# Summing the squares of the SSD branch's outputs on GpSimd over the feature blocks, and on TensorE once at the branch's end

## The chip, the cores and the metric

One core of one Trainium2 chip runs the whole program. The metric is the device time of one execution in microseconds (us). A core has five engines that run side by side: PE (TensorE, matrix products; its weight loads are shown apart as PEld), DVE (VectorE), ACT (ScalarE), POOL (GpSimd) and SP (which only issues DMA transfers here; ACT issues a few as well). Each engine works through its own list of instructions in a fixed order, and waits in place when something that the next instruction needs is not there yet. TensorE's clock has two levels, 1.2 and 2.4 GHz; the profile gives the granted clock as a share of the full one.

## The reference, cut to what matters

The program is a network of five layers over 512 positions of width 1024. The change is in the first layer, in its state-space branch (SSD). That branch gates its output and normalises it over 2048 features:

```python
def ssd_output(y, xs, z, d_skip, g):
    Bsz, L = y.shape[:2]
    y = y + d_skip.reshape(SSD_GROUPS, SSD_HPG, 1).astype(y.dtype) * xs
    return rmsnorm(y.reshape(Bsz, L, D_SSD) * jax.nn.silu(z), g)

def rmsnorm(x, g):
    x32 = x.astype(jnp.float32)
    y = x32 * lax.rsqrt(jnp.mean(x32 * x32, axis=-1, keepdims=True) + EPS)
    return (y * g.astype(jnp.float32)).astype(x.dtype)
```

So each of the 512 positions needs the sum of the squares of 2048 gated features. The factor that comes of it is multiplied in later, behind the branch's output product.

## The kernel before, in words

All is float32. Activations lie with features on the 128 partitions and positions along a row, so 2048 features are 16 blocks of [128, 512]. Large products are made of three products of split operands (`mm3`, lines L101 to L103).

`ssd` handles the branch in four groups of four feature blocks. For each group, `_ssd_project` makes the inputs (PSUM tiles `px`), `_ssd_gate` the gates (`pz`, then `z`), `_ssd_scan` the recurrence over four chunks, forward and backward (state products `pst`, outputs of the state `pof`, diagonal products `pyd`, states `S`, result `y`), and `_ssd_finish` ends the group. While the scan of a group runs, its own gates and the next group's projections are fed in between as filler; in the last group the filler is the attention output product (`pa`) of the class `Mixer`.

`_ssd_finish` does this for each of four blocks j: four transposes of `y` into one PSUM tile `pyT` (the pool `K.pm` has one buffer here), a product with the gate on DVE (L1940), the square on ACT (`sq`, one buffer, L1942), four products on PE that sum the square over the partitions into a [128, 4] tile `pss` (L1944), the scaling by the norm's gain on ACT (L1946), and a write to DRAM (`yd`, issued by ACT, L1947). After the four blocks DVE adds `pss` to `ssy` (L1948). A float32 product is two instructions on PE, so four products show as eight.

When the branch is done, `Mixer.run` turns `ssy` into a row factor (L1997 and after), loads the 16 blocks back (`oin` from `yd`, issued by SP, L1962) and goes on with the weights of the output products.

The order of the instructions on each engine is not written by hand. The framework's scheduler sets it, once, when the program is built, by simulating the whole program in time; so an edit in one place can move instructions in others. Tiles are reused through pools: a new tile waits until the readers of the old one are done. `psum` in `ssd` has one buffer for each tag, and `pst`, `pof` and the chunk product `pcb` share the tag `s`.

Of the kernel before, what the change touches and what calls it, by code (L numbers as in the profile page):

```python
# [9 lines left out]
F32 = mybir.dt.float32  # L10
# [3 lines left out]
ALU = mybir.AluOpType  # L14
# [4 lines left out]
P = 128  # L19
D = 1024  # L20
L = 512
# [1726 lines left out]
def ssd(K, XL, XC, W, V, YD, ssy, last):  # L1748

    nc, tc = K.nc, K.tc
    with ExitStack() as cx:
        pool = cx.enter_context(tc.tile_pool(name="ss", bufs=1))
        psum = cx.enter_context(tc.tile_pool(name="ssp", bufs=1, space=PSUM))
        nc.vector.memset(ssy, 0.0)
        cur = {}
        for _ in _ssd_project(K, pool, XL, XC, W, V, 0, cur):
            pass
        for g in range(4):  # L1760
            nxt, zs = {}, []
            fill = _chain(_ssd_gate(K, pool, XL, W, g, zs), _ssd_project(K, pool, XL, XC, W, V, g + 1, nxt) if g < 3 else last)
            y = pool.tile([P, 4, L], F32, tag="y", bufs=1, name=K.nm("y"))
            for _ in _ssd_scan(K, pool, psum, V, g, cur, y):
                next(fill, None)
            for _ in fill:
                pass
            _ssd_finish(K, pool, psum, V, g, y, zs, YD, ssy)
            cur = nxt


def _chain(*parts):
    for p in parts:
        yield from p
# [49 lines left out]
def _ssd_gate(K, pool, XL, W, g, zs):  # L1824

    nc = K.nc
    for j in range(4):
        w = K.w(W["w_z"][g * 4 + j], [P, KD, P])
        p = K.pg.tile([P, L], F32, tag="g", name=K.nm("pz"))
        K.gemm(p, w, XL, 0)  # L1830
        z = pool.tile([P, L], F32, tag="z", bufs=4, name=K.nm("z"))
        nc.scalar.activation(z, p, AF.Tanh, scale=0.5)
        nc.vector.scalar_tensor_tensor(z, z, 1.0, p, op0=ALU.add, op1=ALU.mult)
        zs.append(z)
        yield
# [93 lines left out]
        yield  # L1929


def _ssd_finish(K, pool, psum, V, g, y, zs, YD, ssy):
    nc = K.nc
    pss = psum.tile([P, 4], F32, tag="q", name=K.nm("pss"))
    for j in range(4):
        z = zs[j]
        pt = K.pm.tile([P, 4, P], F32, tag="m", name=K.nm("pyT"))
        for c in range(4):
            nc.tensor.transpose(pt[:, c, :], y[:, c, j * P:(j + 1) * P], K.ident)
        nc.vector.tensor_tensor(z, pt.rearrange("p a b -> p (a b)"), z, op=ALU.mult)  # L1940
        sq = pool.tile([P, L], F32, tag="sq", bufs=1, name=K.nm("sq"))
        nc.scalar.activation(sq, z, AF.Square)  # L1942
        for c in range(4):
            nc.tensor.matmul(pss[:, c:c + 1], sq[:, c * P:(c + 1) * P], K.ones[:, 0:1],  # L1944
                             start=j == 0 and c == 0, stop=j == 3 and c == 3)
        nc.scalar.activation(z, z, AF.Copy, scale=V["ng"][:, g * 4 + j:g * 4 + j + 1])  # L1946
        nc.scalar.dma_start(YD[g * 4 + j], z)  # L1947
    nc.vector.tensor_tensor(ssy, ssy, pss, op=ALU.add)  # L1948


class Mixer:
# [237 lines left out]
def network(ctx, tc, A, out):  # L2189
# [50 lines left out]
    with ExitStack() as c1:  # L2240
# [33 lines left out]
        with ExitStack() as c2:  # L2274
            K.open_ps(c2, 2, 1)
            K.pump_every, K.pool_w = 2, (2,)
            M = Mixer(K, sub("M"), YD, AD, GD, ssy)
            ssd(K, XL, XC, sub("S"), VS, YD, ssy, M.attention_part(c_x))
# [131 lines left out]
```

## Time and profile before

| | us |
|---|---|
| median of 3 runs | 4372.11 (4363.34 to 4372.17) |
| the profiled execution's own time | 4365.29 |
| its span in the profile | 4363.5 |
| mean granted TensorE clock | 0.952 |
| PE busy | 4007.8 (92%) |
| DVE busy | 2739.3 (63%) |
| ACT busy | 1751.1 (40%) |
| POOL busy | 1507.5 (35%) |

The SSD branch ends at about 1025 us of the span. Busy shares are means over stages that have different limits, and PE's busy time is modelled, since products are pipelined. The sums below are made against the profiled execution, whose own time is 6.8 us under the median.

### The profile page before, as it was taken

How to read it: one execution, taken by the hardware profiler on the slowest of the kernel's cores; microseconds unless marked ns; L12 is line 12 of the kernel's file. 1: busy time of each engine (PE TensorE's matmuls, PEld its weight loads, DVE VectorE, ACT ScalarE, POOL GpSimd, SP SyncE). 2: the span in 40 equal slices, each digit the busy share in tenths (PEclk: the TensorE clock that was granted, in tenths of full speed). 3: DMA queues.
4: the chain of work that ended last, by engine and by line, in shares of the span. 5: the costliest groups of instructions: out<-in, count | busy, mean ns of one | idle time of the engine just before them, and what ended most of it. 6: DMA issues, size and time to landing. Idle time of an engine off the chain costs nothing. (4 is left out here: it accounts for less than half of the span.)

```text
span 4363.5 us, 67568 instructions
## 1 busy us (share of the span) xinstructions
PE 4007.8 (92%) x26396; PEld 3288.7 (75%) x26396; DVE 2739.3 (63%) x4361; ACT 1751.1 (40%) x3331; POOL 1507.5 (35%) x1046
## 2 busy tenths in 40 slices
PE   5888999988989999999988989789989999999999
PEld 3766767656766779888977777577777888888987
DVE  6455476676788884445786687865555466663433
ACT  4445445432233334223343555333323465543321
POOL 4333144443444442222344544534411222211221
PEclk7999999988999999999988998899999999999999
DMA  5113121235444553324534667745512311122222
GB/s 190 60 57 99 54 83 51 85 116 169 145 147 150 168 190 117 97 87 139 174 121 158 222 196 225 188 120 143 139 57 92 102 48 51 53 95 92 90 94 87
DMA packets 345550, 518.45 MB, mean 119 GB/s; under 512 B 114424, under 2 KB 217464, under 8 KB 343696
## 3 DMA queue, kind: packets, MB, share of 16 engines
q1 hardware_dynamic: 339040, 502.08, 37.4%
q10 hardware_dynamic: 6192, 12.06, 0.8%
q8 instruction: 208, 3.41, 0.3%
q14 instruction: 110, 0.90, 0.1%
HBM read 425.86 MB, written 88.19 MB: 118 GB/s over the span
## 5 line engine op out<-in xcount | busy, mean ns | idle before, releaser
L93 POOL TENSOR_TENSOR wlo<-raw,whi 128x1024 fp32r<-128x1024 f32 (+2 forms) x254 | 569.6, 2243 | 1332.8 <-ACT whi L91 960.8
L91 ACT ACTIVATE whi<-raw 128x1024 fp32r<-128x1024 f32 (+3 forms) x399 | 383.4, 962 | 706.4 <-PE pz L102 132.2
L95 DVE TENSOR_TENSOR wlo<-raw,whi 128x1024 fp32r<-128x1024 f32 (+3 forms) x278 | 350.2, 1261 | 288.4 <-ACT whi L91 282.1
L127 DVE SCALAR_TENSOR_TENSOR macc<-mraw,conds,macc 128x1024 f32<-128x1024 f32 x168 | 272.0, 1634 | 36.8 <-DMA mraw<-mw 36.5
L103 PE MATMUL pu<-xh,wlo 128*128 128x512 f32 x608 | 243.0, 400 | 10.3 <-DVE wlo L95 6.5
L102 PE MATMUL pu<-xl,whi 128*128 128x512 f32 x608 | 242.1, 398 | 1.1 <-DVE xl L258 1.1
L101 PE MATMUL pu<-xh,whi 128*128 128x512 f32 x608 | 240.4, 399 | 2.9 <-DVE fu L2063 2.4
L89 DVE CAST whi<-raw 128x1024 fp32r<-128x1024 f32 (+2 forms) x133 | 99.5, 748 | 150.1 <-PE pz L102 46.6
L226 POOL TENSOR_TENSOR rsr<-rsv,mhalf 128x4 f32<-128x4 f32 (+3 forms) x56 | 77.9, 1391 | 276.3 <-DVE rsv L224 258.7
L102 PE MATMUL pz<-xl,whi 128*128 128x512 f32 x384 | 150.0, 391 | 0.0
L101 PE MATMUL pv<-whi,xh 128*128 128x256 f32 x512 | 139.0, 283 | 7.0 <-ACT whi L91 6.2
L103 PEld LDWEIGHTS pu<-xh,wlo 128*128 128x128 f32 x608 | 116.0, 191 | 39.0 <-DVE wlo L95 7.3
L102 PE MATMUL pv<-wlo,xh 128*128 128x256 f32 x512 | 142.1, 282 | 0.0
L103 PE MATMUL pv<-whi,xl 128*128 128x256 f32 x512 | 140.2, 282 | 0.5 <-DVE xl L258 0.5
L101 PEld LDWEIGHTS pu<-xh,whi 128*128 128x128 f32 x608 | 116.1, 191 | 31.8 <-issue 3.5
L102 PEld LDWEIGHTS pu<-xl,whi 128*128 128x128 f32 x608 | 116.0, 191 | 29.1 <-DVE xl L258 1.8
L102 PE MATMUL po<-slo,whi 128*128 128x512 f32 (+1 forms) x384 | 136.1, 357 | 0.0
L103 PE MATMUL po<-shi,wlo 128*128 128x512 f32 (+1 forms) x384 | 135.4, 357 | 0.0
L101 PE MATMUL po<-shi,whi 128*128 128x512 f32 (+1 forms) x384 | 133.9, 364 | 0.5 <-ACT shi L111 0.5
L992 PE MATMUL pgm<-ar,kb 128*128 128x256 f32 x384 | 116.8, 427 | 18.9 <-DMA ar<-fe 15.7
L334 POOL TENSOR_TENSOR u<-u,z 128x512 f32<-128x512 f32 (+1 forms) x48 | 58.5, 1218 | 165.2 <-DVE z L325 165.2
L101 PE MATMUL pl<-xlh,whi 128*128 128x512 f32 x208 | 93.3, 452 | 13.2 <-DVE rp L1488 10.2
(747 smaller groups left out, 12923.8 us busy)
## 6 DMA issues: line engine op xcount, KB each, us to landing
mraw<-mw SPq DMA_DIRECT2D x128, 512.0 KB
raw<-G_wuz SPq DMA_DIRECT2D x96, 512.0 KB
raw<-G_wv SPq DMA_DIRECT2D x48, 512.0 KB
raw<-G_wout SPq DMA_DIRECT2D x48, 512.0 KB
raw<-F_w_up SPq DMA_DIRECT2D x44, 512.0 KB
raw<-R_w_in SPq DMA_DIRECT2D x70, 256.0 KB
raw<-S_w_xbc SPq DMA_DIRECT2D x24, 512.0 KB
fe<-ra SPq DMA_DIRECT2D x16, 768.0 KB
```

Of the source, the lines that this page charges most:

```text
L89: nc.vector.tensor_copy(hi, raw)
L91: nc.scalar.activation(hi, raw, AF.Copy)
L93: nc.gpsimd.tensor_tensor(lo, raw, hi.bitcast(F32), op=ALU.subtract)
L95: nc.vector.tensor_tensor(lo, raw, hi.bitcast(F32), op=ALU.subtract)
L101: nc.tensor.matmul(ps, a[0], b[0], start=start, stop=False)
L102: nc.tensor.matmul(ps, a[0], b[1], start=False, stop=False)
L103: return nc.tensor.matmul(ps, a[1], b[0], start=False, stop=stop)
L127: nc.vector.scalar_tensor_tensor(acc, raw, c[:, kt:kt + 1], acc, op0=ALU.mult, op1=ALU.add)
L226: nc.gpsimd.tensor_tensor(r, v, self.mhalf[:, :n], op=ALU.pow)
L334: nc.gpsimd.tensor_tensor(u, u, z, op=ALU.mult)
L992: nc.tensor.matmul(pgm[:, d], kb[:, i, d, :], ar[:, i, d], start=True, stop=True)
```

## The change

The squares are no longer summed over the partitions one by one. The first block's square is written straight into a new tile `acc` (named `yss`, [128, 512]), and POOL adds each of the other 15 squares to it. After the fourth group four products sum `acc` over the partitions, into a PSUM tile `pss` of the tag `s`, and DVE copies it to `ssy`. The tag `q` of the PSUM pool, the clearing of `ssy` and the four adds to it are gone.

```diff
--- before.py
+++ after.py
@@ -1753,8 +1753,7 @@
     with ExitStack() as cx:
         pool = cx.enter_context(tc.tile_pool(name="ss", bufs=1))
         psum = cx.enter_context(tc.tile_pool(name="ssp", bufs=1, space=PSUM))
-        nc.vector.memset(ssy, 0.0)
-        cur = {}
+        acc, cur = pool.tile([P, L], F32, name="yss"), {}
         for _ in _ssd_project(K, pool, XL, XC, W, V, 0, cur):
             pass
         for g in range(4):
@@ -1765,8 +1764,12 @@
                 next(fill, None)
             for _ in fill:
                 pass
-            _ssd_finish(K, pool, psum, V, g, y, zs, YD, ssy)
+            _ssd_finish(K, pool, V, g, y, zs, YD, acc)
             cur = nxt
+        pss = psum.tile([P, 4], F32, tag="s", name=K.nm("pss"))
+        for c in range(4):
+            nc.tensor.matmul(pss[:, c:c + 1], acc[:, c * P:(c + 1) * P], K.ones[:, 0:1], start=True, stop=True)
+        nc.vector.tensor_copy(ssy, pss)
 
 
 def _chain(*parts):
@@ -1929,23 +1932,21 @@
         yield
 
 
-def _ssd_finish(K, pool, psum, V, g, y, zs, YD, ssy):
+def _ssd_finish(K, pool, V, g, y, zs, YD, acc):
+
     nc = K.nc
-    pss = psum.tile([P, 4], F32, tag="q", name=K.nm("pss"))
     for j in range(4):
         z = zs[j]
         pt = K.pm.tile([P, 4, P], F32, tag="m", name=K.nm("pyT"))
         for c in range(4):
             nc.tensor.transpose(pt[:, c, :], y[:, c, j * P:(j + 1) * P], K.ident)
         nc.vector.tensor_tensor(z, pt.rearrange("p a b -> p (a b)"), z, op=ALU.mult)
-        sq = pool.tile([P, L], F32, tag="sq", bufs=1, name=K.nm("sq"))
+        sq = acc if g == j == 0 else pool.tile([P, L], F32, tag="sq", bufs=1, name=K.nm("sq"))
         nc.scalar.activation(sq, z, AF.Square)
-        for c in range(4):
-            nc.tensor.matmul(pss[:, c:c + 1], sq[:, c * P:(c + 1) * P], K.ones[:, 0:1],
-                             start=j == 0 and c == 0, stop=j == 3 and c == 3)
+        if sq is not acc:
+            nc.gpsimd.tensor_tensor(acc, acc, sq, op=ALU.add)
         nc.scalar.activation(z, z, AF.Copy, scale=V["ng"][:, g * 4 + j:g * 4 + j + 1])
         nc.scalar.dma_start(YD[g * 4 + j], z)
-    nc.vector.tensor_tensor(ssy, ssy, pss, op=ALU.add)
 
 
 class Mixer:
```

In the listings of the changed kernel a line number from L1785 to L1947 is three higher than that of the same line before.

PE, at the end of the first group, from the second group's first state product to the next gate's product `pz`. Before:

```order
L1857 MATMUL pst_5471<-x_1148_5469,BTc_4739 128x512
L1939 MATMUL pyT_5411<-ident,y_4429 128x128 x4
L1857 MATMUL pst_5477<-x_1151_5475,BTc_4739 128x512
L1939 MATMUL pyT_5425<-ident,y_4429 128x128 x4
L1944 MATMUL pss_5410<-ones,sq_5417 128x1 x4
L1857 MATMUL pst_5484<-x_1154_5482,BTc_4739 128x512
L1939 MATMUL pyT_5439<-ident,y_4429 128x128 x4
L1944 MATMUL pss_5410<-ones,sq_5431 128x1 x4
L1857 MATMUL pst_5490<-x_1157_5488,BTc_4739 128x512
L1939 MATMUL pyT_5453<-ident,y_4429 128x128 x4
L1944 MATMUL pss_5410<-ones,sq_5445 128x1 x4
L101 MATMUL pz_5634<-xlh_184,whi_5630 128x512
```

After the change, from the same place:

```order
L1860 MATMUL pst_5455<-x_1146_5453,BTc_4739 128x512
L1942 MATMUL pyT_5410<-ident,y_4429 128x128 x4
L1860 MATMUL pst_5461<-x_1149_5459,BTc_4739 128x512
L1942 MATMUL pyT_5419<-ident,y_4429 128x128 x4
L1860 MATMUL pst_5468<-x_1152_5466,BTc_4739 128x512
L1942 MATMUL pyT_5430<-ident,y_4429 128x128 x4
L1860 MATMUL pst_5474<-x_1155_5472,BTc_4739 128x512
L1942 MATMUL pyT_5441<-ident,y_4429 128x128 x4
L101 MATMUL pz_5618<-xlh_184,whi_5614 128x512
```

The three `pss` rows are gone; a fourth, which stood inside the gate's product, is gone too. The state products `pst` and the transposes `pyT` now follow each other directly.

POOL, at the same place: `x_...` is an input of a state product, `S` a state scaled by its decay. Before:

```order
L1855 TENSOR_TENSOR x_1157_5488<-xTc_4737,wd 128x512
L1862 TENSOR_TENSOR S_5674<-S_5479,ex 128x512
L1862 TENSOR_TENSOR S_5492<-S_5486,ex 128x512
L1862 TENSOR_TENSOR S_6359<-S_5492,ex 128x512
L1909 TENSOR_TENSOR dm_5539<-dm_5539,cbs_5531 128x512
L1909 TENSOR_TENSOR dm_5602<-dm_5602,cbs_5531 128x512
```

After the change:

```order
L1858 TENSOR_TENSOR x_1155_5472<-xTc_4737,wd 128x512
L1865 TENSOR_TENSOR S_5658<-S_5463,ex 128x512
L1947 TENSOR_TENSOR yss<-yss,sq_5425 128x512
L1865 TENSOR_TENSOR S_5476<-S_5470,ex 128x512
L1947 TENSOR_TENSOR yss<-yss,sq_5436 128x512
L1865 TENSOR_TENSOR S_6343<-S_5476,ex 128x512
L1947 TENSOR_TENSOR yss<-yss,sq_5447 128x512
L93 TENSOR_TENSOR wlo_5903<-raw_5900,whi_5902 128x1024
```

The adds into `yss` now stand between the state scalings; one of them stands ahead of `S_5476` (before: `S_5492`), the last state that the second group's start needs. On PE the product `pcb`, with which the second group's first chunk starts, stands behind 24 instructions of the gate's product now; before it stood behind 15.

PE, at the end of the fourth group, from the last filler product `pa` on. Before:

```order
L103 MATMUL pa_8264<-ox_7887,wlo_8272 128x512
L1870 MATMUL pof_8110<-S_8104,CF_6822 128x512
L1857 MATMUL pst_8117<-x_1747_8115,BTl_6820 128x512
L1870 MATMUL pof_8125<-S_8119,CF_6822 128x512
L1939 MATMUL pyT_8301<-ident,y_7531 128x128 x4
L1939 MATMUL pyT_8315<-ident,y_7531 128x128 x4
L1944 MATMUL pss_8300<-ones,sq_8307 128x1 x4
L1939 MATMUL pyT_8329<-ident,y_7531 128x128 x4
L1944 MATMUL pss_8300<-ones,sq_8321 128x1 x4
L1939 MATMUL pyT_8343<-ident,y_7531 128x128 x4
L1944 MATMUL pss_8300<-ones,sq_8335 128x1 x4
L1944 MATMUL pss_8300<-ones,sq_8349 128x1 x4
```

After the change:

```order
L103 MATMUL pa_8220<-ox_7843,wlo_8228 128x512
L1873 MATMUL pof_8051<-S_8045,CF_6792 128x512
L1860 MATMUL pst_8058<-x_1738_8056,BTl_6790 128x512
L1873 MATMUL pof_8066<-S_8060,CF_6792 128x512
L1860 MATMUL pst_8073<-x_1743_8071,BTl_6790 128x512
L1873 MATMUL pof_8081<-S_8075,CF_6792 128x512
L1942 MATMUL pyT_8256<-ident,y_7487 128x128 x4
L1942 MATMUL pyT_8267<-ident,y_7487 128x128 x4
L1942 MATMUL pyT_8278<-ident,y_7487 128x128 x4
L1942 MATMUL pyT_8289<-ident,y_7487 128x128 x4
L1771 MATMUL pss_8300<-ones,yss 128x1 x4
L237 MATMUL prs_8335<-ident,rsr_8333 128x128 x4
```

The sixteen products are four, behind all transposes. Ahead of the transposes one more step of the backward scan (`pst`, `pof`) now stands behind the last filler product.

Elsewhere the scheduler moved instructions as well: up to the end of the feed-forward part that follows, and, among PE's rows 10,000 to 12,700 (the RWKV layer of the second block), in 91 places with some 2,200 of PE's 19,177 rows.

## Rows read from the trace of the kernel before

**Rows 1.** The page's head, busy time by engine over the whole span.
```profile
PE 4007.8 (92%) x26396; PEld 3288.7 (75%) x26396; DVE 2739.3 (63%) x4361; ACT 1751.1 (40%) x3331; POOL 1507.5 (35%) x1046
```

**Rows 2.** Stretches: PE, PEld, DVE, ACT, POOL busy; clock; DMA share; GB/s.
```profile
650.00:672.00 22.00, 20.06 (x92) 13.83 (x92) 11.66 (x20) 8.82 (x17) 12.98 (x12) 0.92 0.21 72
672.00:776.00 104.00, 101.24 (x490) 75.65 (x489) 65.71 (x110) 50.97 (x114) 44.51 (x32) 0.99 0.16 51
...
925.00:1000.00 75.00, 62.62 (x222) 41.37 (x221) 67.50 (x80) 23.55 (x54) 41.16 (x27) 0.84 0.38 127
...
1026.00:1040.00 14.00, 7.15 (x17) 2.56 (x17) 7.51 (x7) 5.19 (x8) 8.67 (x5) 0.50 0.74 263
```

**Rows 3.** Groups by line and form on PE, 640 to 1030 us.
```profile
L1944 PE MATMUL pss<-ones,sq 128*128 128x1 f32 x128 | 18.9, 269 | 0.7 <-ACT sq L1942 0.7
```

**Rows 4.** Timeline of the first group's end: start, length, engine, instruction, [idle before].
```profile
659.58 0.60 PE L1939 MATMUL pyT<-ident,y 128*128 128x128 f32 x4
...
660.02 0.95 PE L1944 MATMUL pss<-ones,sq 128*128 128x1 f32 x8
...
660.34 0.58 ACT L1860 ACTIVATE S<-pst 128x512 f32<-128x512 f32 x1
...
661.05 1.10 PE L1857 MATMUL pst<-x,BTc 128*128 128x512 f32 x2
...
662.42 0.95 PE L1944 MATMUL pss<-ones,sq 128*128 128x1 f32 x8
...
663.24 0.48 PE L101 MATMUL pz<-xlh,whi 128*128 128x512 f32 x1
```

**Rows 5.** The same timeline a little later, inside a gate's product.
```profile
668.21 0.39 PE L103 MATMUL pz<-xlh,wlo 128*128 128x512 f32 x1
...
668.44 0.95 PE L1944 MATMUL pss<-ones,sq 128*128 128x1 f32 x8
...
669.25 0.48 PE L101 MATMUL pz<-xlh,whi 128*128 128x512 f32 x1
```

**Rows 6.** Timeline of the branch's end and the restart after it.
```profile
1006.45 1.02 PE L1870 MATMUL pof<-S,CF 128*128 128x512 f32 x2
...
1010.29 1.13 PE L1870 MATMUL pof<-S,CF 128*128 128x512 f32 x2 [0.85 <-DVE S L1863]
...
1014.96 0.63 ACT L1942 ACTIVATE sq<-z 128x512 f32<-128x512 f32 x1 [27.13 <-DVE z L1940]
...
1017.55 0.63 ACT L1942 ACTIVATE sq<-z 128x512 f32<-128x512 f32 x1 [1.20 <-PE pss L1944]
...
1023.40 1.87 PE L1944 MATMUL pss<-ones,sq 128*128 128x1 f32 x8 [0.72 <-ACT sq L1942]
1024.13 0.33 ACTq L1947 DMA_DIRECT2D yd<-z  x1
1025.31 0.16 DVE L1948 TENSOR_TENSOR ssy<-ssy,pss 128x4 f32<-128x4 f32 x1 [3.53 <-PE pss L1944]
...
1026.60 0.80 SPq L1962 DMA_DIRECT2D oin<-yd  x2
...
1034.73 0.80 PE L101 MATMUL pa<-ox,whi 128*128 128x512 f32 x1 [2.38 <-ACT whi L91]
```

**Rows 7.** Groups by line and form on POOL, 560 to 1060 us.
```profile
L1862 POOL TENSOR_TENSOR S<-S,ex 128x512 f32<-128x512 f32 x28 | 31.7, 1133 | 19.0 <-DVE S L1863 15.2 <-ACT S L1860 3.7
...
L1926 POOL TENSOR_TENSOR y<-y,yo 128x512 f32<-128x512 f32 x16 | 21.4, 1336 | 42.9 <-DVE yo L1872 42.9
...
L2009 POOL TENSOR_TENSOR gs<-gs,rsb 128x512 f32<-128x512 f32 x2 | 3.9, 1988 | 0.0
```

**Rows 8.** Waits of the SP queue, 1000 to 1050 us.
```profile
SPq L1962 <- DMA yd<-z: 53.0, 3, 48.0
```

**Rows 9.** Two later stretches (RWKV layer), columns as in Rows 2.
```profile
2400.00:2800.00 400.00, 343.20 (x3101) 287.13 (x3099) 308.88 (x491) 192.86 (x359) 195.28 (x186) 0.88 0.72 210
2800.00:3300.00 500.00, 450.13 (x6487) 367.68 (x6487) 307.68 (x767) 174.41 (x445) 185.80 (x176) 0.95 0.43 116
```

## The prediction

> **What bounds the kernel now.** I read the page first, then a table of stretches around the SSD branch, then the timeline of the ends of the four groups, then the waits of the SP queue. PE is busy 92% of the span [rows 1], so the first question is whether the removed products stand on a full PE. They do for three groups and not for the fourth. In the end of the first group, 650 to 672 us, PE is busy 20.06 of 22 us, and in the stretch after it 101.24 of 104 [rows 2]: what is taken off PE there moves everything behind it forward. Later it is different. From 925 to 1000 us PE is busy 62.62 of 75 and DVE 67.5 [rows 2], so the fourth group's scan hangs on DVE's work, and at the branch's end PE goes from one short wait to the next: the squares start 2.59 us apart, each waiting until PE has summed the one before [rows 6]. After that PE stands nearly idle until 1034.73, when the first output product starts [rows 6], at half clock (0.50, the 1.2 GHz level) in 1026 to 1040 [rows 2].
>
> The size of the whole matter is small: all 128 `pss` instructions are 18.9 us busy [rows 3], 0.43% of the span.
>
> **Removed: twelve blocks of products in the first three groups.** A block is eight PE instructions. Where one stands in a running product it costs its place in the stream: the product before it starts at 668.21, the block 0.23 later at 668.44, the next product at 669.25 [rows 5]. Without the block that product would start at 668.44, so a block is 0.81 us. One such block stands inside a gate's product in each group, and the other three between state products and transposes. Of those, the last (662.42) stands straight ahead of the next gate's product (663.24) [rows 4], with nothing else to wait for: 0.8 us. The second (660.02) is followed by a state product at 661.05, which shares its PSUM bank with the state that ACT copies away from 660.34 to 660.92 [rows 4]: without the block it could start 0.1 us earlier, perhaps 0.3 if ACT comes sooner. The first I put at the same 0.2. That makes 0.8 + 0.8 + 0.2 + 0.2 = 2.0 us for a group and 6.0 for three. The bounds: if only the block inside the stream counts, 3 x 0.81 = 2.4; if all count in full, 12 x 0.81 = 9.7.
>
> **Added: 15 adds on POOL.** The trace before has the same form in `y<-y,yo`, 1336 ns on average; the shortest kindred group is `S<-S,ex` with 1133 ns and the longest `gs<-gs,rsb` with 1988 ns [rows 7]. I take 1.34 us, the mean of the same form: 20 us of POOL in all. POOL is busy 12.98 of 22 us at a group's end [rows 2], so three or four adds (4.0 to 5.4 us) fit in, but not without order: each stands between state scalings in POOL's list, and one stands ahead of the last state that the next group's scan starts with. The cover is that PE has gate products to do meanwhile, and the listing places the scan's first product `pcb` behind 24 of them (5.6 us at 0.23) instead of 15. The work at the end of each of the first three scans is listed as before, so I cost the late start at nothing; if the scan does not catch up it is about 3 us a group (two adds and a half), 9 for three.
>
> **Added: ACT's wait for POOL.** `sq` has one buffer, so the next square waits for the add. Behind it in ACT's list stand the scaling, the write of `yd`, and the gate's activation, which frees the PSUM bank of a gate product. The wait is up to about 2 us where an add stands behind two scalings (2 x 1133 ns [rows 7]). PE needs that bank only after a further gate product of 24 x 0.23 = 5.6 us; the cover is larger than the wait, so nothing; uncovered it would be 2 us for each group.
>
> **The end of the branch.** Before, squares start at 1014.96 and 1017.55 [rows 6]: one cycle is 2.59 us, at half clock. After, a cycle is square, add and two handovers of about 0.05: 0.63 + 1.34 + 0.10 = 2.07. The fourth square then starts at 1014.96 + 3 x 2.07 = 1021.17 and ends at 1021.80, its add ends near 1023.2, the four products take the 1.87 of a block at this clock [rows 6], and `ssy` is there at 1025.1 instead of 1025.31: 0.2 earlier. More weighs the last write of `yd`. Before, it is issued 0.73 behind the start of the last products (1023.40 and 1024.13), which start as the square ends [rows 6]; so now at 1021.80 + 0.05 + 0.73 = 1022.58, 1.5 earlier. The SP queue holds its reload `oin` for just that write (48 us in its longest wait [rows 8]); the weights of the next product are queued behind it, and PE's restart at 1034.73 behind those. The reload may also have to wait for the memory that `yss` gives back, at 1025.1; against 1026.60 [rows 6] that is 1.5 too. I take 1.5. The bounds come from the adds: with 1.13 us the same reckoning gives 2.2 gained, with 1.99 the reload waits until 1027.7 and 1.1 is lost.
>
> **Moved: one more scan step behind the filler.** In the fourth group a state product and an output of the state now stand behind the last filler product. A step takes 1010.29 - 1006.45 = 3.84 us [rows 6], of which PE's own two products, by the 1.02 of one, are some 1.9 to 2.0. The rest, 1.9 us, was covered by filler before and is not now. It is nothing if the filler that went ahead fills waits of the stretch 925 to 1000, where PE has 12.4 us of idle time [rows 2], and 3.84 if the step is wholly exposed. I take 1.9.
>
> **Everything else that the scheduler moved** I take as 0, because the direction cannot be read from the listing. The bound: in the RWKV stretch PE is idle 56.8 + 49.9 = 106.7 of 900 us [rows 9], and a tenth of that, 10.7 us, won or lost, seems easy with 2,200 rows in other places.
>
> **Sum**: -6.0 - 1.5 + 1.9 = -5.6 us, against the profiled execution 4365.3 - 5.6 = 4359.7. That execution lies 6.8 under the median of the runs shown, so on the median's scale 4366.5. A measurement of this kernel can tell about 0.2%, 8.7 us, from no change; the forecast of -0.13% lies within that.
>
> **A rule that speaks against the change.** At the branch's end, POOL's two-input work on `gs` takes 1988 ns while DVE casts and subtracts weights, against 1336 for the like form `y` [rows 7], so the two engines do hold each other up here. The Trainium skill ("SBUF — State Buffer", Who interferes with whom) says that a DVE instruction with two inputs in SBUF and a GpSimd instruction that reads SBUF shut each other out for a whole instruction. The trace agrees in kind. By that rule all 15 adds could hold DVE 15 x 1.34 = 20 us. By the rows it is far less: in a group's end DVE is busy 11.66 of 22 us [rows 2], and its gate products and state sums there read one input from PSUM. The sum stays.
>
> **The rivals.**
> *All blocks count, or the new order helps later.* For it: PE is full in the first three groups. Against: the state products that follow two blocks have waits of their own. All in full and the scan step hidden: -9.7 - 2.2 = -11.9, so 4360 on the median's scale. With a tenth of the RWKV idle time gone as well: 4349.5. Faster, 0.30.
> *The new order loses later.* One mechanism, one place: in the RWKV stretch PE waits longer since its products and the transfers that feed them stand in another order. For it: 2,200 rows moved and 106.7 us of idle time to grow from. Against: nothing there changed in amount. It decides when it costs 8.7 + 5.6 = 14.3 us, 13% of that idle time; with a fifth, 21 us, the time is 4366.5 + 21 = 4387.5. Slower, 0.13; with less than 13% it ends within 0.2%, which I count in the forecast.
> *The scan starts late and stays late.* POOL's adds ahead of the last state delay `pcb`. At 3 us for each of three groups: -5.6 + 9 = +3.4, 4375.5; slower only from 14.3 us in all, 4.8 a group, which takes adds of 2 us and two of them in the way. 0.10, of which 0.05 slower.
> *It does nothing.* A group's end is a chain of transposes, gate products and states that PE only follows; just the block in the stream counts, and the last group gives back: -2.4 - 0 + 1.9 = -0.5, 4372. 0.10, within 0.2%.
>
> **How the numbers follow.** The forecast (blocks at 2 us a group, later order within 14.3 us) has 0.37, nearly all within 0.2%; its own range is 4360 to 4373. Faster: 0.30 and 0.02 of the forecast, 0.32. Slower: 0.13 + 0.05 = 0.18, and a further 0.01 of the forecast, 0.19. Within: the rest, 0.49. The range reaches from the faster rival with some of the later idle time, 4349, to 4384, short of the slower one's 4387.5; about 1 in 10 is left on each side.
>
> **What the profile after would show.** For the blocks: from the end of the first group's scan (the first `pyT`) to the first gate product, 1 us less, and no gap of 0.81 in the gate's product. For POOL: 15 adds at 1.2 to 1.4 us. For the end: squares 2.1 us apart, the last `yd` issued some 7.6 us after the first square, not 9.2; the last filler product to the first `pyT` about 4 us longer. The prediction is wrong if adds take 2 us, if `pcb` comes later and PE waits in the middle of a group, if the fourth group's order costs more than its 1.9 us, or if the stretches from 1060 us on differ by more than the branch does.

## The result, and the profile after

The changed kernel takes 4393.64 us (median of 4 runs, 4391.27 to 4395.94); the kernel before takes 4368.63 beside it (4 runs, 4363.34 to 4372.17). The ratio is 1.0064 [1.0051, 1.0078]: slower by 0.64%, and 9.6 us above the predicted range. (Ratios here are taken over all runs with a 95% interval; they need not be the quotient of the two medians, which is 1.0057.) The profiled execution took 4395.88 us, with a span of 4394.1 and a mean granted clock of 0.944 (before: 4365.3, 4363.5 and 0.952).

The head of the page of the changed kernel answers to [rows 1]:

```profile
PE 4011.7 (91%) x26276; PEld 3292.7 (75%) x26276; DVE 2748.1 (63%) x4357; ACT 1751.4 (40%) x3331; POOL 1523.3 (35%) x1061
```

PE has 120 instructions fewer and is nevertheless 3.9 us longer busy. The next view is the table of stretches of the changed kernel, with the columns of [rows 2]; it answers to [rows 2, 9]:

```profile
650.00:672.00 22.00, 19.19 (x71) 12.17 (x71) 9.93 (x18) 9.13 (x16) 15.41 (x13) 0.92 0.20 72
...
925.00:1000.00 75.00, 59.33 (x209) 39.91 (x209) 61.12 (x77) 20.00 (x46) 37.97 (x25) 0.89 0.35 114
1026.00:1040.00 14.00, 7.10 (x15) 3.20 (x14) 10.52 (x8) 5.38 (x7) 8.42 (x4) 0.50 0.60 212
...
2800.00:3300.00 500.00, 441.23 (x6411) 362.37 (x6412) 285.92 (x731) 164.23 (x426) 188.32 (x185) 0.91 0.46 117
```

In the branch nothing stands out. In the last row, deep in the RWKV layer, the clock is 0.91 where it was 0.95 [rows 9], and PE gets through fewer instructions in the same 500 us (6411, before 6487). Such windows of fixed time understate a loss, since less work fits into them. So I matched each instruction of the two traces with its fellow (same line, operation and tiles, in order of time) and took the median shift of their starts, by the time before:

```
stretch (us)      changed minus before   what it is
 710 -  730          -1.8                behind the first group's end
 880 -  900          -2.8                behind the second group's end
1026 - 1040          -2.2                end of the branch
1180 - 1220          +4.8                output products of the Mixer
1700 - 1750          +0.8                behind the feed-forward part
2600 - 2650          +0.4                RWKV, features
2800 - 2850         +15.3                RWKV, the scan starts
3000 - 3050         +23.6                RWKV, scan
3100 - 3150         +31.1                RWKV, end of the scan
3300 - 4363         +30.7                all that follows
```

The branch gained 2.2 us. The whole loss came 1600 us later, in a layer in which the change edits nothing, between 2600 and 3130.

What that stretch lost can be split. The windows below are cut at the scan's first product and near the scan's end, so that each holds as many of PE's instructions after as before. Before:

```profile
2600.00:2787.00 187.00, 152.76 (x1552) 128.65 (x1550) 150.41 (x262) 89.94 (x165) 86.33 (x80) 0.84 0.75 212
2787.00:3100.00 313.00, 286.81 (x4680) 230.28 (x4680) 192.40 (x504) 111.29 (x296) 137.96 (x141) 0.96 0.56 141
```

After:

```profile
2604.50:2799.80 195.30, 155.34 (x1553) 130.67 (x1552) 160.80 (x278) 89.45 (x165) 83.74 (x87) 0.81 0.74 209
2799.80:3132.40 332.60, 295.79 (x4680) 240.93 (x4680) 183.99 (x490) 112.33 (x296) 133.50 (x134) 0.91 0.53 131
```

The first is 8.3 us longer, the second 19.6, together 27.9. PE's idle time (span minus busy) grew by 5.7 and 10.6, 16.3 in all. The other 11.6 is PE's busy time, 2.6 and 9.0, for practically the same products: the granted clock fell from 0.84 to 0.81 and from 0.96 to 0.91. Not all of this belongs to the order: e1 (below), which has the order of before, shows clocks of 0.81 and 0.94 in windows cut the same way, and PE is 5.7 us longer busy in them than before.

In the first of them three places can be named, in PE's timeline about the scan's start (start, length, instruction, [idle before <- what ended it]). Before:

```profile
2776.18 2.83 PE L793 MATMUL pM<-ra,bk 64*64 64x64 f32 x48 [14.71 <-DVE bk L785]
2778.93 2.72 PE L823 MATMUL pbo<-r_bones,th 128*64 128x2 f32 x24
2787.32 4.20 PE L992 MATMUL pgm<-ar,kb 128*128 128x256 f32 x8 [5.67 <-DMA ar<-fe]
```

After:

```profile
2781.26 2.83 PE L793 MATMUL pM<-ra,bk 64*64 64x64 f32 x48 [11.57 <-DVE bk L785]
2787.16 2.69 PE L823 MATMUL pbo<-r_bones,th 128*64 128x2 f32 x24 [3.07 <-DVE th L820]
...
2799.84 2.50 PE L992 MATMUL pgm<-ar,kb 128*128 128x256 f32 x5 [9.98 <-POOL ar L955]
```

The last `pM` comes 5.1 us later (the window itself starts 4.5 later), the bonus product `pbo` a further 3.1, the scan's first product `pgm` a further 4.3: 12.5. `pbo` waits because DVE does the product `th` (L820) 13 steps of another inverse (L887 and L889) after `pM`'s operand, where there had been five between. `pgm` waits because POOL clears the operand tiles `ar` of two other segments before those of the first. That is POOL's timeline after; the last row is the first segment's tile:

```profile
2789.92 0.20 POOL L1053 MEMSET S<- 128x128 f32 x1 [10.62 <-PE pbo L823]
2790.18 1.93 POOL L955 MEMSET ar<- 64x1024 f32 x2
...
2797.85 1.93 POOL L955 MEMSET ar<- 64x1024 f32 x2
```

In the scan, PE's longest wait that has no fellow before is for `ks`, which POOL makes of a loaded operand `kb`. In PE's waits of the changed kernel, 2780 to 3040 us, it reads (total, times, longest):

```profile
PE pb L985 <- POOL ks L983: 5.3, 1, 5.3
```

Before, it is 0.7 in that window. SP's timeline after shows where `kb` was:

```profile
2998.51 1.75 SPq L912 DMA_DIRECT2D tt<-tl  x2
3000.35 1.22 SPq L970 DMA_DIRECT2D kb<-fe  x2
```

Ahead of `tt<-tl` SP waits for an earlier transfer out of the tile `tt`, as its waits in 2990 to 3003 us have it:

```profile
SPq L912 <- DMA td<-tt: 4.3, 1, 4.3
```

`kb` needs none of that, but it stands behind it in SP's list.

### The profile page after: what moved, and what is told of

Same layout as the page of the kernel before. It is cut to its first block, busy times and chain, and to the rows that moved or that the text cites. A ratio compares the mean times of both kernels' runs of the same rounds, so it can differ in the third digit from the quotient of the medians.

```text
span 4394.1 us, 67326 instructions
## 1 busy us (share of the span) xinstructions
PE 4011.7 (91%) x26276; PEld 3292.7 (75%) x26276; DVE 2748.1 (63%) x4357; ACT 1751.4 (40%) x3331; POOL 1523.3 (35%) x1061
## 5 line engine op out<-in xcount | busy, mean ns | idle before, releaser
L127 DVE SCALAR_TENSOR_TENSOR macc<-mraw,conds,macc 128x1024 f32<-128x1024 f32 x168 | 262.4, 1579 | 31.3 <-DMA mraw<-mw 31.0
```

The source lines that it names most:

```text
L127: nc.vector.scalar_tensor_tensor(acc, raw, c[:, kt:kt + 1], acc, op0=ALU.mult, op1=ALU.add)
```

## The experiments

My theory (T1): the loss is the order in which the scheduler now lays out the layers behind the branch; the branch itself costs nothing. The rival (T2): the branch with its adds, waits and tiles does it, and the later stretches only carry it on. To tell them apart the order must be set apart from the edit. A helper makes a kernel's instructions follow another kernel's order, engine by engine. It adds order edges alone, which wait for nothing; the table holds the other kernel's order:

```diff
+def follow(tc, start, end, table, engines=("PE", "DVE", "Activation", "Pool", "SP")):
+    traced = tc.nc.cur_bb.bb.instructions
...
+        order = [mine[n] for n in np.cumsum(steps.astype(int))]
...
+        for a, b in zip(order, order[1:]):
+            tc.add_manual_dep(b, a.name, mybir.DependencyInfo(mybir.DependencyClass.NoSync, mybir.DependencyReason.DATA), reason="follow")
```

This is the helper from e5 on; in e1 and e2 it has no `end` and stops where it is called. In the kernels that have it, the lines shown of the later layers have numbers 3 higher. Ratios are to the kernel before on the same chip; the chips differ by some microseconds, so times of different experiments are compared by their ratios.

**e1, the changed branch, and from its end to the end of the RWKV layer the order of before.**

```diff
+    mark = nc.cur_bb.bb.instructions[-1]
...
+    follow(tc, mark, TABLE)
```

> The changed branch, and from its end to the end of the RWKV layer every engine's instructions in the order of the kernel before (order edges alone, no added wait). Theory 1, the loss is the scheduler's other order in the layers behind the branch: the branch's own gain of some 2 us stays and the 28 us of the RWKV layer are gone, so 4363 to 4369 us, 0 to 0.15% faster than before. Theory 2, the loss comes from the branch itself (GpSimd's adds, the late outputs, what it leaves in the queues) and only shows up later: the order makes no difference and the time stays at 4388 to 4396 us. In between (about 4380): both have a part.

Measured: 4366.79 us (12 runs), before 4367.66, ratio 1.0002 [0.9990, 1.0014]. The loss is gone. The branch alone is worth nothing that can be measured; the interval leaves out the predicted -5.6 us (0.9987), not -2.

**e2, the reverse: the branch of before, and behind it the order of the changed kernel.** The same lines in the kernel before, with the other table.

> The kernel before, its branch untouched, with every instruction behind the branch in the order that the changed kernel has there. Theory 1: 4394 to 4399 us, the changed kernel's time and the branch's 1 to 3 us on top, 0.6 to 0.7% slower than before. Theory 2: within 0.2% of before, 4360 to 4377 us.

Measured: 4391.99 (6 runs), ratio 1.0062 [1.0048, 1.0076]. The order alone makes the loss, without one add on POOL; the time is 2 us under what I expected. The table of stretches shows the same in the second window of [rows 9]. e1:

```profile
2800.00:3300.00 500.00, 450.41 (x6480) 368.56 (x6481) 306.91 (x766) 174.17 (x443) 186.30 (x176) 0.94 0.43 116
```

e2:

```profile
2800.00:3300.00 500.00, 439.75 (x6423) 360.47 (x6424) 285.65 (x728) 164.91 (x427) 187.39 (x181) 0.92 0.44 116
```

With the order of before PE is 450.41 us busy of the 500, as before (450.13); with the new order 439.75, as in the changed kernel (441.23).

**e3, the adds on DVE**, which gives the scheduler a third order for everything behind.

```diff
-            nc.gpsimd.tensor_tensor(acc, acc, sq, op=ALU.add)
+            nc.vector.tensor_tensor(acc, acc, sq, op=ALU.add)
```

> The changed kernel with the fifteen adds on VectorE instead of GpSimd. This gives the RWKV layer a third order, unlike both others. Theory 1: the time is not set by where the adds run; anything from 4350 to 4400 us is possible, and the difference to before lies in the RWKV stretch, while the branch ends within 4 us of where it ended before. Theory 2 (GpSimd's adds cost it): at or under the kernel before, 4360 to 4370 us, with the difference in or right behind the branch.

Measured: 4372.96 (12 runs), ratio 1.0014 [1.0001, 1.0027]. By matched instructions it is 8.0 us ahead at the branch's end, 15.0 at 2600, 3.2 at 3000 and 0.6 behind at the end: it too loses some 15 us in the RWKV layer. At the branch's end I had allowed a shift of 4 us, half of what came.

**e4, a control: the kernel before with a second buffer for `sq`,** and nothing else.

```diff
-        sq = pool.tile([P, L], F32, tag="sq", bufs=1, name=K.nm("sq"))
+        sq = pool.tile([P, L], F32, tag="sq", bufs=2, name=K.nm("sq"))
```

> The kernel before with two buffers for the squares instead of one, and nothing else: in the branch worth at most 2 us either way. It changes the order in the RWKV layer as much as the change did. Theory 1: such a neutral edit can move the time by up to 1% through that order alone, either way, and the shift is made in the RWKV stretch. Theory 2: within 0.2% of before, 4360 to 4377 us.

Measured: 4389.26 (6 runs), ratio 1.0052 [1.0037, 1.0066]. An edit that takes no product away and adds no work costs nearly as much as the change. It is 2.0 us ahead at the branch's end, 14.9 behind at 2800 and 19 at the end: the same stretch. With this T2 has fallen.

**e5, the adds on DVE and the RWKV layer in the order of before.** The edit of e3, and `follow` from where the RWKV layer begins.

> The adds on VectorE, and the RWKV layer alone in the order of the kernel before. With its own order the kernel with adds on VectorE reached the RWKV layer 13.4 us ahead of before (profiled runs) and had lost 14 us when it left it. If the order alone makes that loss, the lead is kept: 4351 to 4359 us, 0.2 to 0.4% faster than before, and the fastest so far. Rival: an order fits the moment at which its inputs arrive, and the old one loses the lead too: 4364 to 4374 us.

Measured: 4357.52 (11 runs), before 4364.15, ratio 0.9986 [0.9978, 0.9995]. It is the fastest version: 6 us under the kernel before, and so ahead of both. By matched instructions it is 15.9 us ahead at 2600 and keeps 8.2 of that to the end, so in part the expectation's rival may hold too, that an order fits the moment at which its inputs arrive. The lead is not DVE's doing as far as e8 (below) can tell; it came with another order of the branch, and I have not separated the two there.

**e6 and e7, the loss cut in two at the start of the scan.** Both have the changed branch. e6 has the new order up to the scan and the order of before in it; e7 has the order of before up to the scan and the new one in it. The edits are two further marks for `follow`.

> The changed kernel; only the part of the RWKV layer that is traced from its scan on is put in the order of the kernel before, while all ahead of it (projection, features, first inverses) keeps the changed kernel's order. In the changed kernel's trace the scan's first product starts 12.5 us late, and 18 more are lost in the scan. If each part's order makes its own loss: 12 us of it stay, 4376 to 4384 us. If the order of the features makes all of it (the scan's inputs come in another sequence): 4388 to 4396 us. If the scan's order makes all of it: 4364 to 4370 us.

> The other half: the changed kernel, everything from the branch's end up to the scan in the order of the kernel before, the scan in the changed kernel's order. If each part's order makes its own loss: 4380 to 4390 us (18 us stay). If the features' order makes all of it: 4364 to 4370 us. If the scan's order makes all of it: 4388 to 4396 us.

Measured: e6 4377.68 (11 runs), ratio 1.0026 [1.0016, 1.0037]; e7 4377.11 (11 runs), ratio 1.0031 [1.0022, 1.0039]. Each half of the new order loses by itself, some 11 and 14 us, and the two together, 0.57%, come near the 0.62% of e2. There is no single culprit. e7 ends 3 us under its expected range, and the profiled execution of e6, 4363.80, is the fastest of its runs, so what is said of e6 rests on the other runs.

**e8, e1 without the adds**, so that `yss` holds only the first block's squares and the sum is left incomplete; all other instructions in e1's order.

```diff
-        if sq is not acc:
-            nc.gpsimd.tensor_tensor(acc, acc, sq, op=ALU.add)
```

> Leaves out the fifteen adds: the sum holds the first of the sixteen squared blocks alone. Every other instruction of the branch stands as in the changed kernel, every one behind it as in the kernel before, so it differs from the first experiment (4366.8 us) in fifteen GpSimd instructions and nothing else. As predicted (the adds lie beside other work): within 1.5 us of that experiment in the branch, 4363 to 4369 us in all. Rival (GpSimd delays the scan's last steps, and the four closing products wait 3.1 us for the last add): the branch ends 4 to 7 us earlier, 4358 to 4363 us.

Measured: 4361.94 (11 runs), ratio 0.9998 [0.9989, 1.0007], against 1.0002 of e1. The 19.3 us of work on POOL cost nothing that shows, though the intervals leave room for some 6 us. In microseconds the time lies in the range of the rival, but the kernel before is 3.5 us faster on this chip too, and the branch does not end the 4 to 7 us earlier that the rival asked for. The profiled e8 is 2.6 us ahead of e1 already at 650 us, where the two do not differ yet, and 2.0 at the branch's end: two executions of one order differ by that much, so shifts of 2 to 5 us say nothing.

**e9, the changed kernel in its own order with the three named places repaired.** On POOL the first segment's clearings go ahead of the two other sets, on DVE the bonus product ahead of the twelve inverse steps, on SP the `tt` loads behind the `kb` loads. As the listing of the order has it, the moved rows (- where they stood, + where they stand):

```diff
+POOL MEMSET ar_23947 64x8x128 x2
...
-POOL MEMSET ar_23947 64x8x128 x2
+DVE SCALAR_TENSOR_TENSOR th_23764<-th_23764,r_r_k,r_23301 128x768
...
-DVE SCALAR_TENSOR_TENSOR th_23764<-th_23764,r_r_k,r_23301 128x768
-SP DMA tt<-tl_19736 32x48x32 x2
...
+SP DMA tt<-tl_19736 32x48x32 x2
```

> The changed kernel in its own order with three moves in the RWKV layer, ten instructions in all. GpSimd clears the operands of the scan's first segment ahead of the two other sets it now clears first (6 instructions). VectorE makes the bonus's product as soon as it can, ahead of 12 steps of the triangular inverses. SP issues two loads of one scan segment ahead of the two loads for an inverse, which wait 4.4 us. If the loss is made of such places, where one instruction that TensorE waits for stands behind others on its queue: the waits of 10.0, 3.1 and 5.3 us at these places shrink by 4, 2.5 and 3 to 5 us, in all 8 to 12 us, so 4381 to 4386 us against the changed kernel's 4393.6. Rival, the loss is spread over the whole order (clock, contention) and these waits only move: 4389 to 4396 us.

Measured: 4390.13 (6 runs), ratio 1.0051 [1.0037, 1.0066], against 1.0064 [1.0051, 1.0078]. The intervals overlap, so these runs do not tell the gain of the repairs from nothing; the time is in the range of the rival. PE's waits of e9 in 2780 to 3040 us say why so little came of it:

```profile
PE pgm L995 <- DMA ar<-fe: 12.8, 7, 4.0
...
PE pgm L995 <- DMA kb<-fe: 9.5, 2, 8.1
...
PE pb L988 <- POOL ks L986: 0.9, 1, 0.9
```

The waits for the clearings and for `th` are gone, and 0.9 is left of that for `ks`. But the scan's first product now waits 8.1 us for its `kb` load, which stands behind other transfers on SP: from the last `pM` to that product it takes 13.5 us, where the changed kernel takes 18.6 and the kernel before 11.1. The wait for `ks` has come back as a wait of 4.0 for an `ar` load. Behind each wait stood the next one.

**e10, the same three places spoiled in e1's order.** The rows of e9, moved the other way.

> The first experiment's kernel (changed branch, old order behind it, 4366.8 us) with the same three places spoiled: the first segment's operands cleared behind one more set (6 instructions, 4 us), the bonus's product behind 8 more steps of the inverses (3 us), the two loads of that segment behind the two of the inverse (up to 5 us). If such places make the loss: 4373 to 4379 us. If the loss is spread over the whole order: 4364 to 4370 us.

Measured: 4381.54 (12 runs), ratio 1.0033 [1.0023, 1.0044]: some 13 us above e1, and 2.5 above the upper end of what I expected. By matched instructions e10 goes from some 7 us ahead of e1 at 2750 to 2.6 ahead at 2800, and is 10 to 12 us behind from 3000 on, so most of it arises behind the scan's start, where of the three only the `kb` loads lie. PE's waits of e10 in 2760 to 3040 us have this:

```profile
PE pb L988 <- POOL ks L986: 14.2, 4, 12.8
```

**e11, that place alone: e1 with the two `kb` loads behind the two `tt` loads**, five places of SP's listing later and nothing else.

```diff
-DMA kb<-fe 128x4x128 x2
 DMA v<-tv 32x24x32 x2
 DMA td<-tt 64x3072
...
 DMA tt<-tl 32x48x32 x2
+DMA kb<-fe 128x4x128 x2
```

> The first experiment's kernel (changed branch, old order behind it) with two instructions moved: SP issues the two loads of kb for one scan segment five places later, behind the two loads of tt for an inverse. In the experiment before this one PE waited 12.8 us for that segment's ks in one piece, where the first experiment's kernel did not wait. If that one place made it: 4375 to 4382 us, 10 to 14 us over the first experiment's 4366.8. Rival, the wait came from the two other moves ahead of it, which had shifted the scan against its loads: under 4371 us.

Measured: 4373.47 (8 runs), before 4363.20, ratio 1.0030 [1.0020, 1.0041], that is 0.28% or 12 us above e1, the distance that I expected. (The time itself lies under the expected range; the kernel before is 4.5 us faster on this chip than on that of e1.) SP's timeline of e11:

```profile
2969.97 0.89 SPq L919 DMA_DIRECT2D v<-tv  x2
...
2971.53 4.64 SPq L975 DMA_DIRECT2D ar<-fe  x4
...
2976.93 1.69 SPq L915 DMA_DIRECT2D tt<-tl  x2
2978.66 1.60 SPq L973 DMA_DIRECT2D kb<-fe  x2
```

In e1 it stands so:

```profile
2973.37 0.92 SPq L973 DMA_DIRECT2D kb<-fe  x2
2975.51 0.90 SPq L919 DMA_DIRECT2D v<-tv  x2
```

So `kb` went from 2.1 us ahead of the `v` loads to 8.7 behind them. What PE waits for it, 2960 to 3040 us, e11:

```profile
PE pb L988 <- POOL ks L986: 13.1, 2, 12.6
```

and e1:

```profile
PE pb L988 <- POOL ks L986: 0.6, 2, 0.4
```

The wait of 12.6 us is as large as the price that the runs show. The matched shift confirms the place: e11 is 5.6 us ahead of e1 at 2950 and 6.5 behind at 3000, a step of 12. By 3100 the profiled e11 has won some 4 of them back, so that in these two executions 8 to 9 us stay. In between PE's stretch reads, e1 and then e11:

```profile
2940.00:3020.00 80.00, 74.37 (x1304) 60.74 (x1303) 43.13 (x115) 31.45 (x83) 38.25 (x37) 0.98 0.52 135
```

```profile
2940.00:3020.00 80.00, 64.60 (x1140) 53.29 (x1135) 39.10 (x104) 27.91 (x74) 36.68 (x35) 0.91 0.52 125
```

## Why the prediction was wrong

**The branch was read nearly right.** These rows of the changed kernel's timeline answer to [rows 4, 6]:

```profile
654.92 1.06 PE L1942 MATMUL pyT<-ident,y 128*128 128x128 f32 x4
...
662.08 0.51 PE L101 MATMUL pz<-xlh,whi 128*128 128x512 f32 x1 [0.20 <-DVE z L1836]
...
997.62 1.02 PE L1873 MATMUL pof<-S,CF 128*128 128x512 f32 x2
...
1007.05 2.08 PE L1873 MATMUL pof<-S,CF 128*128 128x512 f32 x2 [0.85 <-DVE S L1866]
...
1011.25 1.12 PE L1942 MATMUL pyT<-ident,y 128*128 128x128 f32 x4 [2.12 <-POOL y L1929]
...
1013.13 0.63 ACT L1945 ACTIVATE sq<-z 128x512 f32<-128x512 f32 x1 [37.80 <-DVE z L1943]
...
1015.15 0.63 ACT L1945 ACTIVATE sq<-z 128x512 f32<-128x512 f32 x1 [0.63 <-POOL yss L1947]
...
1020.58 0.33 ACTq L1949 DMA_DIRECT2D yd<-z  x1
...
1031.50 0.79 PE L101 MATMUL pa<-ox,whi 128*128 128x512 f32 x1 [3.84 <-ACT whi L91]
```

- *Blocks, -2.0 a group.* The first group's end, from the first `pyT` to the gate's product, takes 7.16 us; before it was 8.41 (654.83, which the trace of before shows, to 663.24 in [rows 4]). That is 1.25 less, 1.2 were worked out. With the block inside the gate's product the shift is 1.8, not 2.0. The second group gave only 1.0, and the third cannot be told from the filler that moved. For the two groups that can be read, 2.8 us came where the term of -6.0 has 4.0.
- *The scan step, +1.9.* From the first `pof` behind the last filler product to the first `pyT` it takes 13.6 us (997.62 to 1011.25) and took 7.1 before (1006.45 in [rows 6], to 1013.54): 6.5 more, where "about 4" was expected. In part that is the clock: the granted clock is 0.50 (the 1.2 GHz level) in 1004 to 1012, where it was 1.00 before, and a `pof` takes 2.08 us instead of 1.02. The filler ends 8.8 us earlier, 2.8 of which the second group had brought already, so the step cost a net 0.5. The fourth group's transposes thus start 2.3 us earlier, where -6.0 + 1.9 = -4.1 was forecast.
- *The adds, 1.34 us each, and no wait that matters.* Right; the group of adds on POOL, count | busy, mean ns | idle before:

```profile
L1947 POOL TENSOR_TENSOR yss<-yss,sq 128x512 f32<-128x512 f32 x15 | 19.3, 1285 | 6.3 <-ACT sq L1945 6.3
```

- *The end, squares 2.07 apart, `yd` 7.6 behind the first square.* Measured 2.02 and 7.45. From the first `pyT` to the first output product the gain is 3.2 - 2.3 = 0.9, against 1.5.

In sum the branch gained 2 to 3 us where 5.6 was forecast, no more than two executions of one order differ by. (A slip in the working, 24 x 0.23 = 5.6 us for 5.5, changes nothing.)

**The step that failed** is "Everything else that the scheduler moved I take as 0, because the direction cannot be read from the listing", and with it the bound of 10.7 us, "a tenth" of PE's idle time. The listing had shown 2,200 rows in other places. e1 and e2 show that this term is the whole result: 0.0002 for the branch, 0.0062 for the order. By the profile it is some 33 us, from -2.2 to +30.7. The bound was wrong in kind, too. It counted idle time alone, but 11.6 of the 27.9 us of the stretch were PE's own products at a lower clock, which is not in the idle time at all. How many of the 11.6 the order makes is less sure. In windows cut the same way PE is busy 439.6 us before, and 445.3 (e1) and 438.1 (e8) in the same order; it is busy 451.1 in the changed kernel and 452.6 in e2, which has its order. The prediction had named the sign that came true, that "the stretches from 1060 us on differ by more than the branch does".

**The rival "the new order loses later"** is what happened, in the place and by the mechanism named: "PE waits longer since its products and the transfers that feed them stand in another order". It had 0.13, and its price of 21 us (4387.5) was too small by about 6. Its chance was too low for a reason that the runs show. Three redrawn orders of what lies behind the branch were run (the changed kernel's, e3's, e4's), and from 2600 us to the scan's end all three lost against the order of before, roughly 15 to 30 us. As far as three orders can show it, the order of before is a good one of its kind, and a loss should have been given more than a gain from an edit that redraws it; the prediction had 0.13 for the loss and left the new order's help inside a rival with 0.30.

**The rivals on the branch** (a late scan through the adds, nothing at all) are settled by e8 and e1: the adds cost nothing that shows. The rule of the Trainium skill ("SBUF — State Buffer", Who interferes with whom) that the prediction weighed, by which the adds could hold DVE for 20 us, had no such effect in these runs.

**What stays open.** Of the 27.9 us, the 8.3 up to the scan's start go with three late instructions, and a wait of 5.3 us in the scan with one. e9 shows that these are not the whole cause, since other waits stand behind them. e6 and e7 say that the rest is spread over both halves of the order. That the slower products of the changed order follow from its waits is argued from the clock in the rows, not shown by a run of its own; e4 speaks against it, since it lost 18.8 us in windows cut the same way while PE was 2.7 us less busy in them than before. Why e3's order of the branch is 8 us better is open as well.

## What to carry to other kernels

Where a scheduler lays out the program by simulating it, measure an edit twice, once as it is and once with the rest of the program held to the old order, and run a neutral edit as a control: here the order alone was worth 0.6%, the edit itself nothing that could be measured. When only order has changed, read first the queue that issues the loads, and look for a load that PE's chain needs soon behind loads that could come later or that wait for a buffer. A good order that was found by chance can be kept by pinning it, as e1 and e5 do. A list of late instructions that each have a wait is not yet a list of causes: e9 took three waits away and others stood behind them.

## What the runs showed of the hardware

In e11 two loads came some ten microseconds later, measured against the loads beside them, and that cost 12.6 us of PE's time and 0.28% of the whole program. The DMA share of 0.52 in the rows of e1 and e11 is a mean over 80 us. In the wait itself the DMA engines were full; these are e11's stretches there, with the clock and then the DMA share as the second and third numbers from the right (a packet counts where it starts, so that a short stretch can pass 1):

```profile
2970.00:2975.00 5.00, 1.85 (x44) 1.54 (x42) 2.38 (x7) 1.80 (x4) 0.00 (x0) 1.00 0.86 170
2975.00:2980.00 5.00, 0.00 (x0) 0.00 (x0) 0.00 (x0) 0.00 (x0) 0.00 (x0) 0.51 1.00 215
2980.00:2985.00 5.00, 0.57 (x3) 0.58 (x4) 0.00 (x0) 0.00 (x0) 1.47 (x2) 0.50 1.28 208
2985.00:2990.00 5.00, 5.00 (x67) 3.99 (x65) 1.06 (x4) 2.29 (x6) 4.05 (x5) 0.62 0.26 55
```

From the `v` loads at 2969.97 to the `kb` loads at 2978.66 SP issues nearly without a pause; its waits there come to 0.4 us, so in e11 it is hardly a matter of waiting for a buffer. The `kb` loads were late because of their place in SP's list, and they then had to move on full engines. How much of the 12.6 us either makes, no run separates.

The same rows show the clock in a wait. PE stops at 2971.9; the granted clock falls to 0.51 and 0.50 (the 1.2 GHz level), and after the restart at 2984.4 it is 0.62 and from 2990 on 1.00 again. The Trainium skill ("TensorE: Matmul & The Clock Gate", Part 1: The HAM clock gate) says that the clock depends on how busy PE has been recently; these rows agree. So PE pays for a wait a second time: by matched instructions, what it does in e1 from 2976 to 3020 takes 2.6 us more of its time in e11. That price need not stay: the work from there to 3100 takes 3.2 us less in e11, at a clock of 0.98 instead of 0.94.

The late `pM` showed another cost of order. DVE's timeline before:

```profile
2772.98 1.01 DVE L784 TENSOR_TENSOR ra<-nkk,e 128x256 f32<-128x256 f32 x2
2773.91 1.02 DVE L807 TENSOR_TENSOR ra<-r,e 128x256 f32<-128x256 f32 x2
```

And after:

```profile
2773.63 2.61 DVE L784 TENSOR_TENSOR ra<-nkk,e 128x256 f32<-128x256 f32 x2
2776.16 3.69 DVE L807 TENSOR_TENSOR ra<-r,e 128x256 f32<-128x256 f32 x2
```

The same four instructions take 6.3 us instead of 2.0. Before, POOL was idle beside them; after, its timeline has this:

```profile
2774.79 0.90 POOL L819 TENSOR_TENSOR th<-th,th 128x256 f32<-128x256 f32 x1
2775.65 2.25 POOL L811 TENSOR_TENSOR bk<-th,th 128x768 f32<-128x768 f32 x1
2777.86 1.44 POOL L819 TENSOR_TENSOR th<-th,th 128x512 f32<-128x512 f32 x1
```

The Trainium skill ("SBUF — State Buffer", Who interferes with whom) says that a DVE instruction with two inputs in SBUF and a GpSimd instruction that reads SBUF hold each other up for a whole instruction. The trace agrees, here with a price of 4.3 us, on instructions that stand ahead of the operand that `pM` waits for. It is not enough that POOL is busy: beside one of its clearings (MEMSET, 0.7 us of overlap) the 128x768 form of L784 takes 0.96 us in the trace before, and 0.95 alone. The adds of this change, for which the rule was looked up, paid no such price; the order that they brought about did.
